# The last down-projection stage of a two-block transformer kernel: dummy matmuls, whole weight buffers, other output queues, f32 sum

## The chip, the cores and the metric

The kernel runs on one core of a Trainium2 chip. A core has TensorE (PE) for matmuls, VectorE (DVE), ScalarE (ACT) and GpSimd (POOL) for element-wise work, SyncE (SP), which here only issues transfers, and 16 DMA engines that move data between HBM and the on-chip memory. The metric is the time of one execution on the device in microseconds. All weights come from HBM once per execution.

## The reference

The program computes two transformer blocks for 256 tokens of width 1024 in float32. Each block has a mixer and a mixture of experts; the change touches the experts of the second block alone. There a router picks for each token one of four groups and in it two of eight experts, each expert is a gated network with a hidden width of 512, and its output is added to the token with a weight:

```python
for e in range(N_EXPERTS_2):                       # 32 experts, hidden width 512
    h = jax.nn.silu(t @ w_gate[e]) * (t @ w_up[e])
    y = y + combine[:, e:e + 1] * (h @ w_down[e]).astype(jnp.float32)
return y.astype(xn.dtype).reshape(B, S, D)         # added to the block's input
```

The weights of the second block's experts are 32 x 3 x 1024 x 512 numbers, 201 MB of the 305 MB that the page counts.

## The kernel before

The experts are taken four at a time, in eight groups (`g` from 0 to 7, function `moe`). Every expert has 32 slots for its tokens, so that the four experts of a group fill the 128 rows of TensorE. A 0/1 matrix S, made from the router's choice, gathers the tokens of a group (L1030); the gate and up products (L1156) work on 32 columns of the array for each expert, with weights that stream in; the hidden values are multiplied on DVE (L1073) and transposed (L1081, ACT copy L1083); the down products (L1089) again take 32 columns for each expert; and `combine` puts the result back to the tokens.

In the second block (`n2` is 4) the down products of a group go in four quarters `q` of 256 output columns. One quarter is one weight buffer of 2 MB, four pieces `c` (128 hidden rows for each of the four experts) of 512 KB; each piece takes four products of 128x32 by 128x256, one for each expert, side by side in the array; the trace shows them as 8 rows in two sets of four, since an f32 product passes twice. The quarter's sum stands in half a PSUM bank (`down_room`). `combine` then splits it into a rounded part `yh` (ACT copy, L1055) and the rest `yl` (DVE subtraction, L1056), and multiplies both by the transposed S for the two halves of the tokens (four matmuls, L1063), which add up over all groups in four PSUM banks (`total_`). Only after the last group (`g == 7`) DVE adds these to X (L1067) and the quarter's 256 columns go out, one DMA for each half of the tokens (L1069): the first three quarters from POOL, the last from ACT.

The weights come through SP's queue in the order in which they are used (`order`, `fetch`, `take`): one DMA of 2 MB for a buffer (L882). The last group's four down quarters come from another array, `w_last_2`, which holds the same numbers with the pieces of a quarter behind each other in a row; each piece is a DMA of its own (L872, 16 in all), so that the products of a piece wait for that piece alone. The DMAs of SP take turns over eight semaphores, so each waits until the one eight before it has landed; a DMA also waits until its buffer is free. PE, ACT, DVE and POOL each work through their instructions in the order of the program; a scheduler fixes that order when the program is built. `held` are the four PSUM banks of the second block for the gate (0), the up (1), the down sums (2) and the small work (3); bank 0 is free once the last gate product has been read.

`keep_warm` (L255) runs matmuls of a matrix of ones whose result nobody reads; before the change it is used in other stages alone.

Of the kernel before, what the change touches and what calls it, by code (L numbers as in the profile page):

```python
# [12 lines left out]
F32 = mybir.dt.float32  # L13
# [3 lines left out]
AF = mybir.ActivationFunctionType  # L17
# [4 lines left out]
P = 128  # L22
# [10 lines left out]
WCOLS = 4096  # L33
# [120 lines left out]
def two_blocks(ctx: ExitStack, tc: tile.TileContext, A: dict, at: dict, out: bass.AP):  # L154
    nc = tc.nc
# [83 lines left out]
    ones_b = const.tile([P, P], BF16, name="ones_b")  # L239
# [59 lines left out]
    def tok(tt):  # L299
        return slice(tt * P, (tt + 1) * P)  # L300
# [217 lines left out]
    w = wload(w_in, 8 * IDX, 8, IDX_W, 2)  # L518
# [24 lines left out]
    for tt in range(NT):  # L543
        ps = bank()
# [34 lines left out]
    ps = bank()  # L579
# [12 lines left out]
    for j in range(4):  # L592
        ps = bank()
        nc.tensor.matmul(ps, con("flip"), relH[j // 2][:, j % 2 * 2:j % 2 * 2 + 2, :].rearrange("p h k -> p (h k)"),
                         start=True, stop=True)
# [30 lines left out]
    ps = bank()  # L626
# [37 lines left out]
    ps = bank()  # L664
# [64 lines left out]
    ps = bank()  # L729
# [3 lines left out]
    for c in range(4):  # L733
# [3 lines left out]
        g = t4([P, 4, T])  # L737
# [63 lines left out]
    def moe(route, gI, br, wgate, wup, wdown, wlast, F, final, total):  # L801
# [63 lines left out]

        pieces = LAST_COLUMNS if n2 == 1 else tuple((r, 1) for r in range(n2))

        def wload_columns(c):
            w, r = stream_tile(), []
            for h, n in pieces:  # L870
                v = w[:, h * 1024:(h + n) * 1024]
                nc.sync.dma_start(v, bass.AP(tensor=wlast.tensor, offset=wlast.offset + c * P * WCOLS + h * 1024,  # L872
                                             ap=[[WCOLS, P], [1, n * 1024]]))
                r.append(v.rearrange("p (e n) -> p e n", e=4))
            return r

        def chunk(what, g, c):
            if what == 2 and g == 7:
                return wload_columns(c)
            src = (wgate, wup, wdown)[what]  # L880
            w = stream_tile()
            nc.sync.dma_start(w, bass.AP(tensor=src.tensor,  # L882
                                         offset=src.offset + (g * src.shape[1] + c) * P * WCOLS,
                                         ap=[[WCOLS, P], [1, WCOLS]]))
            if what == 2 and n2 > 1:
                return [w[:, c_ * 1024:(c_ + 1) * 1024].rearrange("p (e n) -> p e n", e=4) for c_ in range(n2)]
            return w.rearrange("p (e n) -> p e n", e=4)
# [164 lines left out]

        def combine(g, ST, yp, col, n):
            yh, yl = (wtile([P, 512], F32R, tag=tag, bufs=2, level="const")[:, :n] for tag in ("sq", "on"))
            nc.scalar.activation(yh, yp[:, :n], AF.Copy)  # L1055
            nc.vector.tensor_sub(yl, yp[:, :n], yh.bitcast(F32))  # L1056
            for tt in R:
                if final:
                    ps = total_[tt][col // 512][:, col % 512:col % 512 + n]
                else:  # L1060
                    ps = bank()[:, :n]
                for i, y in enumerate((yh, yl)):
                    nc.tensor.matmul(ps, ST[:, tok(tt)], y, start=i == 0 and (not final or (g == 0 and col % 512 == 0)),  # L1063
                                     stop=i == 1, skip_group_check=final)
                xs = X[:, tt, col:col + n]
                if not final or g == 7:
                    nc.vector.tensor_add(xs, xs, ps)  # L1067
                if final and g == 7:
                    (nc.scalar if col >= 768 else nc.gpsimd).dma_start(out[0, tok(tt), col:col + n], xs)  # L1069

        def hidden(gu, sg, sc):
            hid = wtile([P, n2, P], tag="on", bufs=2, level="const")
# [13 lines left out]
        def down(g, hT_, ST):  # L1086
            def step(yp, j, c, w):
                js = slice(32 * j, 32 * j + 32)
                nc.tensor.matmul(yp[js], hT_[:, c, js], w, start=c == 0, stop=c == n2 - 1)  # L1089

            if n2 > 1:
                for q in range(4):
                    w = take(2, g, q)
                    yp = down_room()
                    for c in range(n2):
                        for j in range(4):
                            step(yp[:, :256], j, c, w[c][:, j])
                    combine(g, ST, yp, q * 256, 256)
            elif g < 7:
                yp = [acc() for _ in range(2)]  # L1100
                for c in range(n2):
                    w = take(2, g, c)
                    for hf in range(2):
                        for j in range(4):
                            step(yp[hf], j, c, w[:, j, hf * 512:(hf + 1) * 512])
                for hf in range(2):
                    combine(g, ST, yp[hf], hf * 512, 512)
            else:
                for (h, n), w in zip(pieces, take(2, g, 0)):
                    yp = acc()  # L1110
                    for j in range(4):
                        step(yp[:, :256 * n], j, 0, w[:, j])
                    combine(g, ST, yp, h * 256, 256 * n)
# [220 lines left out]
def prepare(inputs):  # L1334
# [12 lines left out]
    for x in ("", "_2"):  # L1347
        for n in ("w_gate", "w_up", "w_down"):
# [3 lines left out]
            else:  # L1352
                if x:
# [3 lines left out]
    w = a["w_down"][0, 28:].reshape(4, P, D)  # L1357
    arrays["w_last"] = np.concatenate([w[:, :, h * 256:(h + n) * 256].transpose(1, 0, 2).reshape(P, -1)
                                       for h, n in LAST_COLUMNS], 1)[None]
    w = a["w_down_2"][0, 28:].reshape(4, P, 4, 4, 256)  # L1360
    arrays["w_last_2"] = np.ascontiguousarray(w.transpose(3, 1, 2, 0, 4)).reshape(4, P, WCOLS)
    return arrays, at


# [15 lines left out]
```

## Time and profile before

| | us |
|---|---|
| median of 3 runs | 929.75 (928.58 to 931.29) |
| the profiled execution, total | 927.07 |
| its span, first to last instruction | 925.4 |
| mean granted clock of TensorE over the span | 0.92 of 2.4 GHz |
| busy in the span: PE, DVE, ACT, POOL | 760.7, 348.0, 264.7, 172.2 |

The span is what the trace shows; the total of the same execution is 1.67 us longer. A row of the timeline gives start, duration, engine, line, operation, output and inputs, the form, and how many instructions it merges; PE is matmuls, PEld weight loads, an engine's name with q at its end stands for its sequencer, which waits and issues. In brackets is the idle time of the engine before the row and what ended it. The granted clock is a share of 2.4 GHz: 1.00 is 2.4 GHz and 0.50 is 1.2 GHz.

### The profile page before, as it was taken

What the parts mean: (1) busy time and instruction counts of PE and PEld (TensorE: products, weight loads), DVE (VectorE), ACT (ScalarE), POOL (GpSimd) and SP (SyncE); (2) the same over time, 40 slices, a digit from 0 to 9 for tenths busy, and PEclk for the clock granted to TensorE, in tenths of its full rate; (3) what the DMA queues carried; (4) which work ended last, traced back from release to release, by engine and by line L of the source; (5) the groups of instructions that cost most, each with busy time, mean ns of one, the idle gap of its engine ahead of it and who ended that gap; (6) DMA issues with size and microseconds to landing.
All of it is one profiled execution on the core that took longest, in us unless ns stands there. A gap on an engine that the chain in (4) does not pass through costs nothing.

```text
span 925.4 us, 14953 instructions
## 1 busy us (share of the span) xinstructions
PE 760.7 (82%) x6166; PEld 491.3 (53%) x6166; DVE 348.0 (38%) x776; ACT 264.7 (29%) x615; POOL 172.2 (19%) x163
## 2 busy tenths in 40 slices
PE   7989999999998988898999976576486676758666
PEld 6768899986766766786874532132141322313212
DVE  4956465575554558668582110010010101101002
ACT  6446655544211164564651100000000000000000
POOL 3422354575000046522240000000000000000001
PEclk9899999999999998999999997998788968988877
DMA  9561535667599984424669999999999999999996
GB/s 369 228 227 75 200 122 243 252 262 305 216 425 426 419 366 182 188 92 149 259 251 420 428 429 427 425 428 427 426 425 427 427 428 429 428 426 427 426 419 255
DMA packets 26639, 305.04 MB, mean 330 GB/s; under 512 B 2936, under 2 KB 4728, under 8 KB 8512
## 3 DMA queue, kind: packets, MB, share of 16 engines
q1 hardware_dynamic: 25984, 302.93, 79.3%
q8 instruction: 50, 0.82, 0.4%
q0 software_dynamic: 288, 0.79, 0.2%
q10 hardware_dynamic: 288, 0.26, 0.1%
q14 instruction: 29, 0.24, 0.1%
HBM read 302.91 MB, written 1.06 MB: 328 GB/s over the span
## 4 chain that ended last, share of the span: by engine, by line
DMA 44%; PE 17%; DVE 5%; ACT 2%; issue 1%; POOL 1%; DVEq 0%; ACTq 0%; SPq 0%; POOLq 0%
DMA w<-w_up 16%; DMA w<-w_gate 13%; DMA w<-w_down 13%; PE acc L291 6%; DMA w<-w_last 2%; PE ps L1156 2%; PE acc L1156 2%; PE ps L1030 1%; PE ps L1063 1%; PE ps L467 1%; PE acc L1089 1%; POOL wlo L286 1%; PE ps L460 1%; ACT b L446 1%; ACT whi L285 0%
## 5 line engine op out<-in xcount | busy, mean ns | idle before, releaser
L1156 PE MATMUL ps<-w,XT 128*32 128x512 f32 x1024 | 159.3, 748 | 71.9 <-DMA w<-w_up 42.5
L286 POOL TENSOR_TENSOR wlo<-w,whi 128x512 fp32r<-128x512 f32 (+3 forms) x115 | 144.8, 1270 | 190.8 <-ACT whi L285 156.2
L285 ACT ACTIVATE whi<-w 128x512 fp32r<-128x512 f32 (+3 forms) x208 | 120.4, 590 | 91.3 <-PE acc L291 76.9
L1156 PEld LDWEIGHTS ps<-w,XT 128*32 128x32 f32 x1024 | 30.9, 123 | 169.9 <-DMA w<-w_up 68.8
L286 DVE TENSOR_TENSOR wlo<-w,whi 128x512 fp32r<-128x512 f32 (+3 forms) x93 | 71.4, 771 | 54.5 <-ACT whi L285 51.6
L291 PE MATMUL acc<-whi,aT_hi 128*128 128x512 f32 (+3 forms) x240 | 89.2, 377 | 1.0 <-issue 0.7
L291 PE MATMUL acc<-whi,aT_lo 128*128 128x512 f32 (+3 forms) x240 | 87.1, 368 | 0.0
L1089 PE MATMUL ps<-w,pT 128*32 128x256 f32 x1024 | 72.0, 424 | 14.5 <-DMA w<-w_down 11.6
L1069 POOL DMA_DIRECT2D out<-X x6 | 3.4, 577 | 431.4 <-DVE X L1067 431.4
L291 PE MATMUL acc<-wlo,aT_hi 128*128 128x512 f32 (+3 forms) x240 | 70.3, 371 | 5.8 <-DVE wlo L286 3.4
L1083 ACT ACTIVATE pT<-ps 128x128 f32<-128x128 f32 (+1 forms) x16 | 7.0, 437 | 193.3 <-PE ps L1081 193.3
L1030 PE MATMUL ps<-S,X 128*128 128x128 f32 x256 | 39.0, 296 | 23.5 <-DVE XT L1033 12.8
L1030 PEld LDWEIGHTS ps<-S,X 128*128 128x128 f32 x256 | 32.8, 199 | 42.7 <-DVE XT L1033 20.7
L1073 DVE SCALAR_TENSOR_TENSOR on<-ps,sc,sq 128x512 f32<-128x512 f32 x8 | 8.8, 1097 | 123.7 <-PE ps L1156 123.7
L1056 DVE TENSOR_TENSOR on<-ps,sq 128x256 fp32r<-128x256 f32 x32 | 13.6, 425 | 109.3 <-ACT sq L1055 109.3
L1089 PEld LDWEIGHTS ps<-w,pT 128*32 128x32 f32 x1024 | 31.7, 118 | 43.1 <-DMA w<-w_down 14.1
L291 PEld LDWEIGHTS acc<-whi,aT_hi 128*128 128x128 f32 x240 | 46.8, 195 | 11.2 <-issue 3.0
L1033 DVE TENSOR_TENSOR XT<-ps,ck 128x256 f32<-128x256 f32 (+1 forms) x48 | 24.6, 512 | 71.5 <-PE ps L1030 71.4
L291 PEld LDWEIGHTS acc<-wlo,aT_hi 128*128 128x128 f32 x240 | 43.4, 194 | 14.3 <-DVE wlo L286 4.4
L1055 ACT ACTIVATE sq<-ps 128x256 fp32r<-128x256 f32 x32 | 12.3, 384 | 134.6 <-PE ps L1089 134.6
L291 PEld LDWEIGHTS acc<-whi,aT_lo 128*128 128x128 f32 x240 | 46.7, 194 | 6.8 <-issue 0.9
L1045 ACT ACTIVATE ST<-ps 128x256 fp32r<-128x256 f32 x16 | 6.1, 384 | 131.3 <-PE ps L1042 131.3
(288 smaller groups left out, 1190.5 us busy)
## 6 DMA issues: line engine op xcount, KB each, us to landing
w<-w_up SPq DMA_DIRECT2D x40, 2048.0 KB, 39.1
w<-w_gate SPq DMA_DIRECT2D x40, 2048.0 KB, 39.1
w<-w_down SPq DMA_DIRECT2D x35, 2048.0 KB, 39.1
w<-w_in SPq DMA_DIRECT2D x13, 2048.0 KB, 10.3
w<-w_last SPq DMA_DIRECT2D x18, 512.0 KB, 12.8
w<-w_out SPq DMA_DIRECT2D x4, 2048.0 KB, 7.4
w<-w_in SPq DMA_DIRECT2D x2, 1056.0 KB, 19.7
w<-w_in SPq DMA_DIRECT2D x2, 1040.0 KB, 14.6
```

Of the source, the lines that this page charges most:

```text
L285: turn[1] = nc.scalar.activation(r[0], v, AF.Copy)
L286: eng.tensor_sub(r[1], v, r[0].bitcast(F32))
L291: nc.tensor.matmul(out_, a, b, start=start, stop=stop, **kw)
L446: nc.scalar.activation(prob[:, r, s], src, AF.Exp, bias=bias[:, 2 * s + r:2 * s + r + 1], accum_out=sm[:, h:h + 1])
L460: nc.tensor.transpose(ps[:, q * P:(q + 1) * P], prob[:, r, s, tok(kt)], ident)
L467: nc.tensor.matmul(o[:, h * 64:(h + 1) * 64], pT[:, q * P:(q + 1) * P], v[:, kt, h * 64:(h + 1) * 64], start=kt == 0, stop=kt == tt)
L1030: nc.tensor.matmul(ps[:, kk * n:(kk + 1) * n], h[:, tt, kp + kk, :], S[:, tt].rearrange("p e s -> p (e s)"), start=i == 0, stop=i == len(t ...
L1033: nc.vector.tensor_mul(XT[kp * gn // 8][:, k:k + 2, :], ps[:, :2 * n].rearrange("p (k s) -> p k s", k=2), gI[:, kp:kp + 2, None].to_broadc ...
L1055: nc.scalar.activation(yh, yp[:, :n], AF.Copy)
L1056: nc.vector.tensor_sub(yl, yp[:, :n], yh.bitcast(F32))
L1089: nc.tensor.matmul(yp[js], hT_[:, c, js], w, start=c == 0, stop=c == n2 - 1)
L1156: mm = nc.tensor.matmul(gu[i][32 * j:32 * j + 32, :F], XT[k * gn // 8][:, k % (8 // gn), (g % gn) * P + 32 * j:(g % gn) * P + 32 * j + 32] ...
```

## The change

Four things change, all in the last group of the second block's experts.

- The first two down quarters of the last group come as whole buffers of 2 MB from `w_down_2`, like those of the other groups; only the last two come in pieces. The array `w_last_2` now is a copy of those two quarters.
- After each piece's products of the last group, except the last piece of all, PE runs two matmuls of ones (128x512 in bf16) into the free bank `held[0]`: 15 times two. `keep_in_program_order` holds them in their place.
- The output DMAs of the first three quarters are collected and issued by SP, behind the last weight's DMA. Of the last quarter's two, the first stays on ACT and the second goes to POOL.
- The last quarter's sum is not split: ACT copies 128 of its columns and DVE the other 128 in f32, and two f32 matmuls replace the four.

```diff
--- before.py
+++ after.py
@@ -865,17 +865,19 @@
 
         pieces = LAST_COLUMNS if n2 == 1 else tuple((r, 1) for r in range(n2))
 
+        last_load, outs = [None], []
+
         def wload_columns(c):
             w, r = stream_tile(), []
             for h, n in pieces:
                 v = w[:, h * 1024:(h + n) * 1024]
-                nc.sync.dma_start(v, bass.AP(tensor=wlast.tensor, offset=wlast.offset + c * P * WCOLS + h * 1024,
+                last_load[0] = nc.sync.dma_start(v, bass.AP(tensor=wlast.tensor, offset=wlast.offset + (c + wlast.shape[0] - n2) * P * WCOLS + h * 1024,
                                              ap=[[WCOLS, P], [1, n * 1024]]))
                 r.append(v.rearrange("p (e n) -> p e n", e=4))
             return r
 
         def chunk(what, g, c):
-            if what == 2 and g == 7:
+            if what == 2 and g == 7 and c >= n2 - wlast.shape[0]:
                 return wload_columns(c)
             src = (wgate, wup, wdown)[what]
             w = stream_tile()
@@ -1052,21 +1054,36 @@
 
         def combine(g, ST, yp, col, n):
             yh, yl = (wtile([P, 512], F32R, tag=tag, bufs=2, level="const")[:, :n] for tag in ("sq", "on"))
-            nc.scalar.activation(yh, yp[:, :n], AF.Copy)
-            nc.vector.tensor_sub(yl, yp[:, :n], yh.bitcast(F32))
+            plain = final and g == 7 and col == 768
+            if plain:
+                nc.scalar.activation(yh[:, :128].bitcast(F32), yp[:, :128], AF.Copy)
+                nc.vector.tensor_copy(yh[:, 128:].bitcast(F32), yp[:, 128:n])
+            else:
+                nc.scalar.activation(yh, yp[:, :n], AF.Copy)
+                nc.vector.tensor_sub(yl, yp[:, :n], yh.bitcast(F32))
             for tt in R:
                 if final:
                     ps = total_[tt][col // 512][:, col % 512:col % 512 + n]
                 else:
                     ps = bank()[:, :n]
-                for i, y in enumerate((yh, yl)):
+                if plain:
+                    nc.tensor.matmul(ps, ST[:, tok(tt)].bitcast(F32), yh.bitcast(F32), start=False, stop=True,
+                                     skip_group_check=True)
+                for i, y in enumerate(() if plain else (yh, yl)):
                     nc.tensor.matmul(ps, ST[:, tok(tt)], y, start=i == 0 and (not final or (g == 0 and col % 512 == 0)),
                                      stop=i == 1, skip_group_check=final)
                 xs = X[:, tt, col:col + n]
                 if not final or g == 7:
                     nc.vector.tensor_add(xs, xs, ps)
                 if final and g == 7:
-                    (nc.scalar if col >= 768 else nc.gpsimd).dma_start(out[0, tok(tt), col:col + n], xs)
+                    if col < 768:
+                        outs.append((out[0, tok(tt), col:col + n], xs))
+                    else:
+                        (nc.gpsimd if tt else nc.scalar).dma_start(out[0, tok(tt), col:col + n], xs)
+                        if not tt:
+                            with tc.issue_after(last_load[0].ins):
+                                for o, x in outs:
+                                    nc.sync.dma_start(o, x)
 
         def hidden(gu, sg, sc):
             hid = wtile([P, n2, P], tag="on", bufs=2, level="const")
@@ -1095,6 +1112,11 @@
                     for c in range(n2):
                         for j in range(4):
                             step(yp[:, :256], j, c, w[c][:, j])
+                        if g == 7 and q * n2 + c < 4 * n2 - 1:
+                            for _ in range(2):
+                                tc.keep_in_program_order(
+                                    nc.tensor.matmul(held[0], ones_b, ones_b[:, None, :].to_broadcast([P, 4, P]),
+                                                     start=True, stop=True))
                     combine(g, ST, yp, q * 256, 256)
             elif g < 7:
                 yp = [acc() for _ in range(2)]
@@ -1357,8 +1379,7 @@
     w = a["w_down"][0, 28:].reshape(4, P, D)
     arrays["w_last"] = np.concatenate([w[:, :, h * 256:(h + n) * 256].transpose(1, 0, 2).reshape(P, -1)
                                        for h, n in LAST_COLUMNS], 1)[None]
-    w = a["w_down_2"][0, 28:].reshape(4, P, 4, 4, 256)
-    arrays["w_last_2"] = np.ascontiguousarray(w.transpose(3, 1, 2, 0, 4)).reshape(4, P, WCOLS)
+    arrays["w_last_2"] = np.ascontiguousarray(arrays["w_down_2"][7, 2:])
     return arrays, at
 
 
```

TensorE, the last quarter of the last group, before. The names with a number are one buffer each: `w` the weights, `pT` the transposed hidden values, `ps_5628` the down sums, `acc` the sums over the groups, `sq` and `on` the two parts of the split sum.

```order
L1089 MATMUL ps_5628<-w_7629,pT_7528 32x256 x16
L1063 MATMUL acc_5623<-sq_7650,ST_7473 128x256
L1063 MATMUL acc_5625<-sq_7650,ST_7473 128x256
L1063 MATMUL acc_5623<-on_7651,ST_7473 128x256
L1063 MATMUL acc_5625<-on_7651,ST_7473 128x256
L1376 UNCONDITIONAL_BRANCH
```

The same place in the changed kernel, from the third piece of the quarter on; `ps_5626` is the bank `held[0]`.

```order
L1106 MATMUL ps_5628<-w_7641,pT_7528 32x256 x4
L1118 LDWEIGHTS ones_b_82
L1118 MATMUL ps_5626<-ones_b_82 128x512
L1118 LDWEIGHTS ones_b_82
L1118 MATMUL ps_5626<-ones_b_82 128x512
L1106 MATMUL ps_5628<-w_7641,pT_7528 32x256 x4
L1070 MATMUL acc_5623<-sq_7668,ST_7473 128x256
L1070 MATMUL acc_5625<-sq_7668,ST_7473 128x256
L1397 UNCONDITIONAL_BRANCH
```

Between two pieces PE now has two loads of the ones and two matmuls with them; the combine is two matmuls instead of four.

SP's queue from the last up buffer to its end, before:

```order
L882 DMA w_7512<-w_up_2 128x4096
L872 DMA w_7530<-w_last_2 128x1024 x4
L872 DMA w_7563<-w_last_2 128x1024 x4
L872 DMA w_7596<-w_last_2 128x1024 x4
L872 DMA w_7629<-w_last_2 128x1024 x4
L1376 UNCONDITIONAL_BRANCH
```

And in the changed kernel:

```order
L884 DMA w_7512<-w_up_2 128x4096
L884 DMA w_7530<-w_down_2 128x4096
L884 DMA w_7566<-w_down_2 128x4096
L874 DMA w_7602<-w_last_2 128x1024 x4
L874 DMA w_7641<-w_last_2 128x1024 x4
L1086 DMA out<-X_64 128x256 x6
L1397 UNCONDITIONAL_BRANCH
```

Two DMAs of 2 MB stand where eight of 512 KB stood, and six output DMAs follow the last weight. Before these places, the engines' instructions are the same in both kernels but for their line numbers.

## Rows read from the trace of the kernel before

**Rows 1.** The head of the page: span and number of instructions.

```profile
span 925.4 us, 14953 instructions
```

**Rows 2.** The chain of waits from 860 us: start, duration, engine and line.

```profile
896.78 10.61 DMA w<-w_last
...
918.82 1.12 PE ps L1089 x8
...
919.97 0.39 ACT sq L1055
...
920.41 0.86 PE acc L1063 x3
...
921.29 0.42 DVE X L1067
```

**Rows 3.** Stretches: length, busy PE, PEld, DVE, ACT, POOL, clock, DMA share, GB/s.

```profile
860.00:880.00 20.00, 13.09 (x94) 4.47 (x93) 0.61 (x2) 0.52 (x2) 0.00 (x0) 0.83 1.01 427
...
900.00:905.00 5.00, 3.75 (x47) 2.12 (x51) 0.69 (x2) 0.98 (x2) 0.00 (x0) 1.00 1.03 409
...
916.00:918.00 2.00, 2.00 (x20) 0.80 (x24) 0.56 (x2) 0.00 (x0) 1.07 (x2) 0.50 0.40 158
```

**Rows 4.** Timeline of the last group's down stage, from 901 us.

```profile
901.35 1.93 PE L1089 MATMUL ps<-w,pT 128*32 128x256 f32 x32 [0.69 <-ACT pT L1083]
903.41 0.38 ACT L1055 ACTIVATE sq<-ps 128x256 fp32r<-128x256 f32 x1 [2.11 <-PE ps L1089]
...
903.84 0.50 PE L1063 MATMUL acc<-sq,ST 128*128 128x256 f32 x2 [0.56 <-ACT sq L1055]
...
904.74 1.64 PE L1089 MATMUL ps<-w,pT 128*32 128x256 f32 x24
905.47 1.29 POOL L1069 DMA_DIRECT2D out<-X  x2 [422.67 <-DVE X L1067]
...
909.99 0.20 PEld L1089 LDWEIGHTS ps<-w,pT 128*32 128x32 f32 x8 [0.37 <-DMA w<-w_last]
...
911.87 0.20 PEld L1089 LDWEIGHTS ps<-w,pT 128*32 128x32 f32 x8 [1.68 <-DMA w<-w_last]
...
913.14 0.20 PEld L1089 LDWEIGHTS ps<-w,pT 128*32 128x32 f32 x8 [1.08 <-DMA w<-w_last]
...
915.81 0.75 DVE L1067 TENSOR_TENSOR X<-X,acc 128x256 f32<-128x256 f32 x2 [0.67 <-PE acc L1063]
...
916.52 1.07 POOL L1069 DMA_DIRECT2D out<-X  x2 [5.27 <-DVE X L1067]
...
921.29 0.75 DVE L1067 TENSOR_TENSOR X<-X,acc 128x256 f32<-128x256 f32 x2 [0.48 <-PE acc L1063]
921.74 0.86 ACTq L1069 DMA_DIRECT2D out<-X  x2
```

**Rows 5.** DMA issues around 917 and 922.5 us: count, KB each, us to landing.

```profile
out<-X POOLq DMA_DIRECT2D x2, 128.0 KB, 2.6
...
out<-X ACTq DMA_DIRECT2D x2, 128.0 KB, 1.9
```

**Rows 6.** Matmuls of ones before: timeline, and durations (ns min/median/max).

```profile
482.40 3.40 PE L255 MATMUL acc<-ones_b 128*128 128x512 bf16 x15
...
L255 PEld LDWEIGHTS <-ones_b x38: 95/98/291, 227.6 to 486.7; 128*128 128x128 bf16 x38
L255 PE MATMUL acc<-ones_b x38: 376/379/634, 227.8 to 486.9; 128*128 128x512 bf16 x38
```

**Rows 7.** Timeline of PE where 32-column and full-width matmuls alternate.

```profile
843.72 1.06 PE L1156 MATMUL ps<-w,XT 128*32 128x512 f32 x8
844.72 0.66 PE L1081 MATMUL ps<-zk,on 128*128 128x128 f32 x4
845.31 1.06 PE L1156 MATMUL ps<-w,XT 128*32 128x512 f32 x8
```

**Rows 8.** Groups by form over the span: busy us, mean ns, idle before.

```profile
L1083 ACT ACTIVATE pT<-ps 128x128 f32<-128x128 f32 x8 | 2.2, 278 | 29.6 <-PE ps L1081 29.6
```

## The prediction

> **What bounds the kernel now.** I read the chain of waits first. In its last stretch it is DMA almost alone: the weight stream holds it up to 918.82 us, and then come 1.12 us of down products, 0.39 of ACT, 0.86 of combining matmuls and 0.42 of DVE [rows 2]. So the tail counts as weights first, then a serial finish. The span is 925.4 us [rows 1]; the profiled execution took 927.07, 1.67 us more.
>
> The table by stretches says what the engines do in that tail. The granted clock of TensorE is 1.00 (2.4 GHz) at 900 to 905 us and 0.50 (1.2 GHz) at 916 to 918, after weight loads had waited 0.37 to 1.68 us for pieces between 909.99 and 913.14; the DMA engines are full at 900 and only 0.40 busy at 916 to 918 [rows 3, 4]. The timeline gives the steps [rows 4]: a quarter of down products takes 1.93 us at full clock, ACT reads it 0.13 us after its end (901.35 + 1.93 to 903.41) and needs 0.38, the combine starts at 903.84 and the next quarter at 904.74. At half clock the last piece alone takes 1.12 us.
>
> The finish after the last product: the ACT copy, the combine at 920.41, two DVE adds from 921.29 (the second ends at 922.04), two issues on ACT from 921.74, the second starting at about 922.2 and landing 1.9 us later [rows 2, 4, 5]. That is 924.1; the span ends 1.3 us behind it.
>
> **The change, part by part.**
>
> *Two quarters as whole buffers, and the outputs behind the weights.* With 16 KB rows the stream moves 427 GB/s, with the 4 KB rows of the pieces 409 [rows 3]. A quarter is 2.10 MB, 4.92 us against 5.13, so two whole quarters save 0.4 us. The outputs leave POOL's queue, where there are three pairs of one pattern, issued beside the weights [rows 4]. Between 909.99 and 911.87 a piece took 1.88 us, between 911.87 and 913.14 1.27, with 0.5 MB in both [rows 4]; I put the 0.6 down to the first pair. Two pairs can delay weights that still have to land (the third is issued at 916.52), so about 1.2 us goes. The last weight lands at 918.8 - 0.4 - 1.2 = 917.2 (918.8 if I am wrong on the outputs). The six issues that SP takes over stand behind its last weight, so nothing on SP waits for them but the end of the program. The last two depend on the third quarter's adds and would land before 922 us even with a POOL landing (2.6 us), earlier than the last quarter's own outputs. I cost them at nothing.
>
> A whole buffer also has a price: PE can begin a quarter only when all of it has landed. The first lands near 901.7 (the last up buffer had landed by 896.78 [rows 2], plus 4.92), where PE began at 901.35 [rows 4]: 0.35 us. The second is there at 907.0 (its last piece landed two pieces of 1.27 before 909.99 [rows 4], at 907.4, less the 0.4), where PE used to begin it at 904.74 on its first pieces. The early start is lost.
>
> *Dummy matmuls.* After each of the 15 first pieces PE runs two 128x512 bf16 matmuls. Fifteen such matmuls in a row took 3.40 us [rows 6]; less the 0.38 of a single one that is 0.216 each, 0.43 a pair, at full clock. They are in PE's order, so a landed piece waits behind them. A piece's own products are 2 sets of 0.22 (the quarter's 1.93 less a tail of 0.16, over 8 sets), together 0.43. Then there is the change of weights, twice a piece. The row of ones_b has 98 ns for a load [rows 6], and in a place where 32-column products and full-width ones alternate, 843.72 to 845.31 is 1.59 us [rows 7] against 2 sets of 0.43 and four transposes of 0.11, which leaves 0.29 for two changes. So a change costs between 0 (hidden) and 0.15; I take 0.10, the load's own row. One piece is then 0.43 + 0.43 + 0.20 = 1.06 us (bounds 0.86 and 1.15).
>
> The Trainium skill, "TensorE: Matmul & The Clock Gate", Step-by-step, says that PE pulls weight loads ahead of matmuls in flight, so that the next tile's weights load during this one's matmul. By that rule the changes cost nothing and a piece is 0.86. The rows at 843.72 to 845.31 do not agree with it for two shapes that alternate.
>
> A quarter that starts at s has its last products done at s + 3 x 1.06 + 0.60 and lets the next start 0.13 + 0.38 + 0.05 + 0.90 later, at s + 5.24. The dummies behind its fourth piece end at s + 4.24, before the combine could start (s + 4.34), and cost nothing. From 901.7 the first quarter is through at 906.9, so the second starts with its weights at 907.0. The third starts at 912.24 and the fourth at 917.48; by then all weights have landed. The last product ends at 917.48 + 3.18 + 0.60 = 921.26 us, against 918.82 + 1.12 = 919.94 before. PE becomes the bound: +1.3 us.
>
> *The last quarter in f32.* ACT and DVE each copy 128 columns instead of 256 on ACT and a subtraction behind it. ACT's 128x128 row is 278 ns [rows 8]; DVE adds 256 columns in 0.42 [rows 2], and half of them should not take it longer than ACT. I take 0.28 against 0.38, a gain of 0.1 (bounds 0 and 0.15). The subtraction was hidden by the first two combining matmuls, so its removal gives nothing. Two f32 matmuls replace four in f32r. f32 work passes twice, and a pass over 256 columns is the 0.22 of a set, so 4 x 0.22 plus 0.27 of lead and tail is 1.15 us to the last result, where before the second add began 1.22 after the combine's start. Gain 0.07 (bounds -0.2 and +0.2). Together the second add ends at 921.26 + 0.13 + 0.28 + 0.05 + 1.18 + 0.41 = 923.31.
>
> *The last output on POOL.* Before, ACT issued both, and the second landed 2.05 us after the second add. POOL starts its issue later: its pair at 916.52 starts 0.29 after the end of the first add (915.81 + 0.42) [rows 4], and it landed after 2.6 us where ACT's took 1.9 [rows 5]. Part of the 2.6 may be the weights that were still moving, so I take 2.2 between the two rows: 0.29 + 2.2 = 2.5, a loss of 0.45 (bounds 0.1 and 0.85). ACT's own output is earlier and hidden.
>
> The Trainium skill, "DMA: Bandwidth & Descriptors", Latency and other measured facts, gives about 600 ns to the first byte for a queue of ACT or SP and about 1 us for one of POOL. By its 0.4 us the loss would be 0.7 with POOL's later start. The rows, 1.9 and 2.6, point the same way, by more.
>
> **Sum.** Last product +1.3, copy -0.1, combine -0.05, output +0.45, together about +1.7 us: span 927.1, execution 928.8. The median of the runs is 929.75, 2.7 above the profiled execution; I put the +1.7 on it: **931.5 us**.
>
> **Rivals.**
>
> *The weight changes are hidden*, by the skill's rule above. Then a piece is 0.86, the last product ends at 907.0 + 9 x 0.86 + 4.72 = 919.46, 0.5 before now, and the total with -0.15 and +0.45 is -0.2: 929.6 us. For it: in PE's own streams loads do hide. Against it: the 0.29 of rows 7, where shapes alternate as here.
>
> *The clock falls all the same*, the one that ends on the other side. PE still waits for the second quarter until 907.0, and before the change the clock stood at 0.50 at 916 to 918 [rows 3]. If it falls as early as 907, each of about 11 pieces pays double for products and dummies, 0.86 us more, so +9 us: 940. It is over 0.3% slower from 4 such pieces on. Against it: with the dummies PE is near full from 901.7 on, and at 900 to 905, with 3.75 of 5 us busy, it held 1.00.
>
> *PE keeps up with the weights*, so that only the earlier landing counts: last weight 917.2 instead of 918.8, the last piece 0.59 instead of 1.12, -2.1 in all; with -0.15 and +0.45, -1.8: 927.9. It needs the dummies to cost nothing on PE's path, against the 0.43 a pair of rows 6. That the dummies keep the clock and yet bring nothing, since their own time is what the clock gives back, is my forecast itself.
>
> **How the numbers follow.** Forecast 0.68, hidden changes 0.20, falling clock 0.05, PE keeping up 0.07. A difference of 0.3% is 2.8 us, about what a measurement of this kernel can tell from no change. The forecast's own range is from the bounds of the pieces (0.86 to 1.15, -1.8 to +0.8 us) and of the output (-0.35 to +0.4), which seldom meet: 929.6 to 932.7. Medians of three runs of the same kernel wander too (928.58 to 931.29 for the single ones), and the range takes in the two rivals below: 928.6 to 933.4. Slower by over 0.3% (above 932.5) takes the falling clock and the upper end of the forecast, 0.05 + 0.10; faster by over 0.3% (below 927.0) is a part of the last rival and chance, 0.05; the rest, 0.80, is within.
>
> **What would show it.** Right: granted clock 1.00 through 901 to 921; the last weight landing near 917 and no piece of the last quarter waited for; pieces about 1.06 us apart on PE; the second quarter starting at 907; the last product ending near 921.3; the second add about 2.05 us later; the last output landing 2.5 us after that. Wrong: a chain that still ends in the weights' DMA (PE keeps up), pieces at 0.86 (hidden), or a clock of 0.50 in the last quarters.

## The result and the profile after

The changed kernel is slower. In five runs beside five of the kernel before, its median is 936.66 us (932.64 to 940.18) against 930.64. The ratio of the two is 1.0079, with a 95% interval of 1.0051 to 1.0106. On the 929.75 us of before this is +7.3 us (+4.7 to +9.9); the forecast was +1.7 us, and its range ended at 933.4. A later set of ten runs gave 1.0071 (1.0048 to 1.0093). The profiled execution took 932.64 us, the lowest of its five runs, against 927.07 before.

The head of the page and the busy row answer to [rows 1] and to the small table ahead.

```profile
span 930.8 us, 15009 instructions
...
PE 762.6 (82%) x6196; PEld 493.0 (53%) x6196; DVE 346.6 (37%) x776; ACT 264.6 (28%) x615; POOL 170.3 (18%) x158
```

To compare one profile with another, a common zero is needed. Every kernel here has the same instructions up to the products of the last up buffer, but for the matmuls of ones that three of them have in the up stage; and yet these products start between 895.6 and 902.0 us in the fourteen profiles. That spread is none of the change's doing. So I count from that start to the end of the span and call it the tail. In before the start is this row of the timeline:

```profile
896.81 1.92 PE L1156 MATMUL ps<-w,XT 128*32 128x512 f32 x16 [1.29 <-DMA w<-w_up]
```

The tail of before is 925.4 - 896.81 = 28.6 us. After, it is 930.8 - 897.00 = 33.8. Here is the timeline of PE after, from the same row on (start, duration, line, operation, form, count, idle time before and its releaser):

```profile
897.00 3.38 PE L1178 MATMUL ps<-w,XT 128*32 128x512 f32 x16 [1.25 <-DMA w<-w_up]
...
903.01 0.76 PE L1106 MATMUL ps<-w,pT 128*32 128x256 f32 x8 [0.69 <-ACT pT L1100]
903.70 1.03 PE L1118 MATMUL ps<-ones_b 128*128 128x512 bf16 x2
904.66 1.08 PE L1106 MATMUL ps<-w,pT 128*32 128x256 f32 x8
...
907.27 0.60 PE L1118 MATMUL ps<-ones_b 128*128 128x512 bf16 x2
...
909.89 0.64 PE L1106 MATMUL ps<-w,pT 128*32 128x256 f32 x8
...
911.00 0.64 PE L1106 MATMUL ps<-w,pT 128*32 128x256 f32 x8
...
915.25 0.64 PE L1106 MATMUL ps<-w,pT 128*32 128x256 f32 x8
...
920.60 0.64 PE L1106 MATMUL ps<-w,pT 128*32 128x256 f32 x8
...
923.92 0.64 PE L1106 MATMUL ps<-w,pT 128*32 128x256 f32 x8
924.63 0.28 ACT L1059 ACTIVATE sq<-ps 128x128 f32<-128x128 f32 x1 [4.97 <-PE ps L1106]
924.94 0.29 DVE L1060 COPY sq<-ps 128x128 f32<-128x128 f32 x1 [3.59 <-ACT sq L1059]
925.29 1.13 PE L1070 MATMUL acc<-sq,ST 128*128 128x256 f32 x4 [0.72 <-DVE sq L1060]
926.02 0.85 DVE L1077 TENSOR_TENSOR X<-X,acc 128x256 f32<-128x256 f32 x2 [0.79 <-PE acc L1070]
...
927.18 0.74 POOL L1082 DMA_DIRECT2D out<-X  x1 [443.92 <-DVE X L1077]
```

These rows answer to [rows 4]. First look for brackets: behind 903.01 no product of the down stage waits for a transfer. PE is the bound now, as forecast. Then look at the distances. A whole quarter runs from 909.89 to 915.25 and from 915.25 to 920.60, which is 5.36 and 5.35 us. But the first one takes from 903.01 to 909.89, 6.88 us: its first pieces have 1.03 us for two dummies where later ones have 0.60, and 1.08 for products where later ones have 0.64. The stretches say why (columns as in [rows 3]):

```profile
895.00:900.00 5.00, 3.75 (x20) 0.60 (x16) 0.00 (x0) 0.00 (x0) 0.00 (x0) 0.50 1.01 429
900.00:903.00 3.00, 1.04 (x8) 0.42 (x4) 1.09 (x1) 0.60 (x1) 0.00 (x0) 1.00 0.98 415
903.00:905.00 2.00, 1.99 (x14) 0.49 (x18) 0.00 (x0) 0.00 (x0) 0.00 (x0) 0.60 1.00 408
905.00:907.00 2.00, 2.00 (x18) 0.33 (x10) 0.00 (x0) 0.00 (x0) 0.00 (x0) 0.55 0.99 391
907.00:910.00 3.00, 2.97 (x28) 1.08 (x24) 0.54 (x2) 0.39 (x1) 0.00 (x0) 1.00 1.02 406
...
915.00:920.00 5.00, 5.00 (x44) 1.48 (x44) 1.06 (x3) 0.38 (x1) 0.00 (x0) 1.00 0.33 119
```

The granted clock is 0.50 (1.2 GHz) while PE multiplies the last up buffer. It is 1.00 at 900 to 903, where PE is busy for 1.04 of 3 us and otherwise waits for DVE and ACT. It is 0.60 and 0.55 at 903 to 907, in the first pieces, with PE full, and 1.00 from 907 on. The transfers thin out from 915 on. The last weight landed at 916.9 (issued at 906.81, with 10.1 us to landing), and PE finished its last product 7.7 us behind it.

```profile
w<-w_last SPq DMA_DIRECT2D x1, 512.0 KB, 10.1
...
out<-X POOLq DMA_DIRECT2D x1, 128.0 KB, 2.2
```

The second of these rows is the last output (the answer to [rows 5]): issued by POOL at 927.18, landed 2.2 us later.

### The profile page after: what moved, and what is told of

Its sections match the earlier page's. It is cut to its first block, busy times and chain, and to the rows that moved or that the text cites. A ratio compares the mean times of both kernels' runs of the same rounds, so it can differ in the third digit from the quotient of the medians.

```text
span 930.8 us, 15009 instructions
## 1 busy us (share of the span) xinstructions
PE 762.6 (82%) x6196; PEld 493.0 (53%) x6196; DVE 346.6 (37%) x776; ACT 264.6 (28%) x615; POOL 170.3 (18%) x158
## 3 DMA queue, kind: packets, MB, share of 16 engines
HBM read 302.91 MB, written 1.06 MB: 327 GB/s over the span
## 4 chain that ended last, share of the span: by engine, by line
issue 48%; PE 14%; DVE 5%; ACT 2%; POOL 1%; POOLq 0%; ACTq 0%; another core or an unknown queue 0%; DVEq 0%
PE acc L291 6%; PE acc L1178 2%; PE ps L1073 1%; PE ps L467 1%; PE ps L1032 1%; PE acc L1106 1%; POOL wlo L286 1%; PE ps L460 1%; ACT b L446 1%; ACT whi L285 0%; DVE hss L373 0%; PE ps L430 0%; PE ps L389 0%; DVE wlo L286 0%; DVE rs_t L332 0%
## 5 line engine op out<-in xcount | busy, mean ns | idle before, releaser
L1178 PE MATMUL ps<-w,XT 128*32 128x512 f32 x1024 | 154.1, 726 | 74.7 <-DMA w<-w_up 46.9
L1082 POOL DMA_DIRECT2D out<-X x1 | 0.7, 740 | 443.9 <-DVE X L1077 443.9
```

Of the source, the lines that this page charges most:

```text
L1178: mm = nc.tensor.matmul(gu[i][32 * j:32 * j + 32, :F], XT[k * gn // 8][:, k % (8 // gn), (g % gn) * P + 32 * j:(g % gn) * P + 32 * j + 32] ...
```

## The experiments

The theory after the result: the dummies make PE the bound, by their own time and by the first quarter at half clock. The rivals: one of the other three edits costs it, or the delay lies ahead of the down stage. Each part of the change was undone or made alone, then the number of dummies and the clock at the stage's start were changed. All ratios are to the kernel before, run beside it; the tail is that of the one profiled execution.

| kernel | median us | ratio (95%) | tail us |
|---|---|---|---|
| before | 929.76 to 930.64 | 1 | 28.6 |
| the changed kernel | 936.66 | 1.0079 (1.0051 to 1.0106) | 33.8 |
| without dummies | 929.32 | 1.0002 (0.9981 to 1.0024) | 26.8 |
| dummies alone | 935.3 | 1.0073 (1.0047 to 1.0099) | 33.0 |
| whole buffers alone | 929.8 | 0.9995 (0.9974 to 1.0016) | 27.2 |
| output queues alone | 929.02 | 0.9996 (0.9970 to 1.0021) | 27.1 |
| f32 sum alone | 929.55 | 1.0003 (0.9980 to 1.0026) | 27.7 |
| changed, one dummy for two | 932.33 | 1.0029 (1.0010 to 1.0049) | 31.1 |
| before, dummies in the up stage | 929.5 | 0.9987 (0.9969 to 1.0005) | 27.6 |
| changed, dummies in the up stage too | 932.18 | 1.0028 (1.0008 to 1.0048) | 31.3 |
| best, with up dummies | 927.22 | 0.9965 (0.9948 to 0.9983) | 25.9 |
| best, without them | 927.16 | 0.9976 (0.9955 to 0.9998) | 25.9 |
| the changed kernel again | 936.87 | 1.0071 (1.0048 to 1.0093) | 33.7 |
| sum split by rows, no dummies | 929.18 (one run) | - | 26.3 |

**The dummies taken out of the changed kernel, and put alone into the one before.**

```diff
-                        if g == 7 and q * n2 + c < 4 * n2 - 1:
-                            for _ in range(2):
-                                tc.keep_in_program_order(nc.tensor.matmul(held[0], ones_b, ...))
```

> The changed kernel without its 30 dummy matmuls; all else stays. Theory: the dummies, each ahead of landed pieces in PE's order, make PE the bound of the last stage and so let the clock with which PE enters it count in full. Without them a piece is 0.43 us at 2.4 GHz and 0.85 at 1.2 GHz, and PE ends within a microsecond or so of the last weight (916.9 in the changed kernel): 928 to 931 us, 5 to 8 below the changed kernel's 936.7, and a spread over the runs like that of before (about 3 us). Rival one, the whole buffers (PE cannot begin the second quarter before 907): still slower than before, 934 or more. Rival two, the outputs that moved to SP and POOL: still slower, 934 or more.

> The kernel before with the dummy matmuls alone. Theory: PE is the bound, about 1.1 us a piece at 2.4 GHz and twice that at 1.2: 934 to 937 us, most of what the whole change costs, with a wide spread over the runs. Rivals (whole buffers, outputs): within 1 us of before.

Without them the time is that of before, 1.0002; alone they cost 1.0073, nearly the whole. The spreads were not as I expected: the seven runs with the dummies alone lie within 2.8 us, the twelve without them within 6.8. The timeline of PE without dummies:

```profile
904.64 3.43 PE L1106 MATMUL ps<-w,pT 128*32 128x256 f32 x32 [0.69 <-ACT pT L1100]
...
909.50 1.93 PE L1106 MATMUL ps<-w,pT 128*32 128x256 f32 x32
...
917.42 0.64 PE L1106 MATMUL ps<-w,pT 128*32 128x256 f32 x8 [0.20 <-DMA w<-w_last]
918.68 0.64 PE L1106 MATMUL ps<-w,pT 128*32 128x256 f32 x8 [0.62 <-DMA w<-w_last]
```

Its first quarter runs at half clock too (3.43 us against 1.93 for the second), but the last pieces wait for their transfers again, so that the end follows the weights and the slow quarter costs nothing. With the dummies alone, the first products of the four quarters stand at these rows:

```profile
905.33 0.91 PE L1089 MATMUL ps<-w,pT 128*32 128x256 f32 x8 [0.69 <-ACT pT L1083]
...
912.28 0.64 PE L1089 MATMUL ps<-w,pT 128*32 128x256 f32 x8
...
917.63 0.64 PE L1089 MATMUL ps<-w,pT 128*32 128x256 f32 x8
...
922.99 0.64 PE L1089 MATMUL ps<-w,pT 128*32 128x256 f32 x8
```

The first quarter takes 6.95 us, the next two 5.35 and 5.36: the same steps as in the changed kernel, with none of its other edits.

**The three other edits, each alone in the kernel before.**

```diff
...
-            if what == 2 and g == 7:
+            if what == 2 and g == 7 and c >= n2 - wlast.shape[0]:
...
```

> The kernel before with its first two last-group quarters as whole buffers, nothing else. Theory: the weights end 0.4 us earlier, PE begins the second quarter at about 907 instead of 904.7 but has time to catch up: within 1 us of before. Rival (whole buffers are the cause): 933 us or more.

```diff
-                    (nc.scalar if col >= 768 else nc.gpsimd).dma_start(out[0, tok(tt), col:col + n], xs)
+                    if col < 768:
+                        outs.append((out[0, tok(tt), col:col + n], xs))
...
+                        (nc.gpsimd if tt else nc.scalar).dma_start(out[0, tok(tt), col:col + n], xs)
```

> The kernel before with the outputs of the first three quarters on SP behind the last weight and the last output on POOL, nothing else. Theory: the last weight lands about 1.2 us earlier (917.6 instead of 918.8), POOL's last output gives 0.5 back: 929 to 931 us, at most 1 us from before. Rival (the outputs are the cause): 933 us or more.

```diff
+            if plain:
+                nc.scalar.activation(yh[:, :128].bitcast(F32), yp[:, :128], AF.Copy)
+                nc.vector.tensor_copy(yh[:, 128:].bitcast(F32), yp[:, 128:n])
...
```

> The kernel before with the last quarter summed in f32 alone. Theory: the ACT copy shortens by 0.1 us, but DVE's copy waits for ACT's and adds 0.3, and the combine is as long as before: no gain, within 1 us of before. From the last product's end to the second add's end 2.4 us against 2.1 before.

None can be told from before; the medians lie within 0.8 us of each other. The landing of the last weight, counted from the landing of the last up buffer, tells more: 21.6 us with the f32 sum alone, whose stream is that of before (22.0 there), 21.2 with whole buffers, 20.3 with the outputs elsewhere, and 19.9 with both, in one profile each. So whole buffers save about 0.4 us and the outputs about 1.3, the sizes of the forecast. The f32 sum doesn't shorten the finish: from the end of the last product to that of the second add it takes 2.31 us, and 2.14 with the split sum (up-stage dummies alone). DVE's copy starts only when ACT's has ended, as at 924.63 and 924.94 after.

**One dummy for two in the changed kernel.**

```diff
-                            for _ in range(2):
+                            for _ in range(1):
```

> The changed kernel with one dummy matmul after each piece instead of two. Theory: the price is by the dummy on PE's path: a piece is 0.43 + 0.22 + 0.2 to 0.25 for two changes of weights, about 0.88 us instead of 1.11 at 2.4 GHz. From the second quarter on, PE gains 12 x 0.22 = 2.6 us, and some more where the clock is low in the first: 932 to 934.5 us. Rival (the dummies' number does not matter, only that PE switches weights at all): within 1 us of the changed kernel's 936.

```profile
909.87 0.64 PE L1106 MATMUL ps<-w,pT 128*32 128x256 f32 x8
910.44 0.39 PE L1118 MATMUL ps<-ones_b 128*128 128x512 bf16 x1
910.76 0.64 PE L1106 MATMUL ps<-w,pT 128*32 128x256 f32 x8
```

A piece now takes 0.89 us (909.87 to 910.76); with two dummies it was 1.11 (909.89 to 911.00). So a dummy is 0.22, as forecast, and what is left of 0.89 behind one dummy and the products' 0.43 is 0.24: two changes of weights, 0.12 each on average. They don't hide. The ratio falls to 1.0029.

**Dummies in the up stage, in the kernel before and in the changed one.** They keep PE busy where it waits for the last up buffer, and change nothing behind it.

```diff
+                        if final and g == 7 and i == 1:
+                            for _ in range(10 if c < n1 - 1 else 4):
+                                tc.keep_in_program_order(nc.tensor.matmul(held[0], ones_b, ...))
```

> The kernel before with the 34 dummy matmuls in its up stage alone. Theory: its end follows the last weight, so a higher clock at the start of the down stage gives at most 0.5 us at the last piece: within 1 us of before. Rival (the clock at the start bounds the kernel before too): 2 us or more below before.

> The changed kernel with 34 more dummy matmuls in the up stage of the last group (10 behind each of the first three buffers' products, 4 behind the last), where PE waits 2 to 3 us for every buffer. Theory: the changed kernel's slow first quarter (6.9 us where 2.4 GHz gives 5.4, and a start 1.3 us late) and its spread come from a clock of 1.2 GHz as PE enters the down stage. With PE kept busy ahead of it the clock is 1.00 there, the first quarter takes 5.4 us and the median falls by 3 us or more against the changed kernel, to 930 to 933.5. Rival (the clock at the start is no matter, the dummies in the down stage are all): within 1 us of the changed kernel.

In the kernel before they bring nothing that can be told (0.9987, interval to 1.0005). In the changed one they take the ratio from 1.0071 to 1.0028. Its timeline of PE, and a stretch (columns as before):

```profile
897.87 1.92 PE L1178 MATMUL ps<-w,XT 128*32 128x512 f32 x16 [0.61 <-DMA w<-w_up]
...
902.86 0.64 PE L1106 MATMUL ps<-w,pT 128*32 128x256 f32 x8 [1.12 <-DMA w<-w_down]
...
908.28 0.64 PE L1106 MATMUL ps<-w,pT 128*32 128x256 f32 x8
```

```profile
903.00:907.00 4.00, 4.00 (x40) 0.94 (x34) 0.00 (x0) 0.06 (x1) 0.00 (x0) 1.00 0.99 405
```

The clock is 1.00 in the first quarter, which takes 5.42 us (902.86 to 908.28) instead of 6.88, and the last up products take 1.92 instead of 3.38. The first quarter now waits for its whole buffer, landed 902.86 - 897.87 = 5.0 us behind the last up buffer, as forecast (4.92). This is the stage as I had forecast it, and the kernel then costs +2.6 us (+0.7 to +4.5), where I had said +1.7.

**What the other edits are worth without the dummies.** In the changed kernel the down dummies go, the two f32 halves get a buffer and two matmuls each, so that the first half's matmuls don't wait for DVE, and the second last output goes to SP. It was run with the up dummies and without.

```diff
-                nc.vector.tensor_copy(yh[:, 128:].bitcast(F32), yp[:, 128:n])
+                nc.vector.tensor_copy(yl[:, :128].bitcast(F32), yp[:, 128:n])
...
-                        (nc.gpsimd if tt else nc.scalar).dma_start(out[0, tok(tt), col:col + n], xs)
+                        (nc.sync if tt else nc.scalar).dma_start(out[0, tok(tt), col:col + n], xs)
```

> No dummies in the down stage, the 34 in the up stage; whole buffers and outputs behind the weights as in the change; the last quarter's two f32 halves in two buffers (so that DVE need not wait for ACT) and its second output on SP instead of POOL. Theory: PE enters at 2.4 GHz and keeps up with the weights, the end follows the last weight: from the last up buffer's landing to the end about 26.3 us, against 28.6 in the kernel before and 26.8 without any dummies; 926.5 to 929 us, up to 0.4% below before. Rival (low clock does no harm once the dummies are gone from the down stage): the same as the next kernel.

> The kernel just above without the 34 dummies in the up stage. Theory: where the clock is low at the start PE is behind the weights at first and catches up, so it costs at most 1 us against the kernel above: 927 to 930 us. DVE's copy starts together with ACT's instead of 0.3 us after it.

Both beat before by a little, 0.9965 and 0.9976, and can't be told apart: the up dummies aren't needed. They don't keep the clock up for long either. The second quarter with them:

```profile
909.93 3.36 PE L1107 MATMUL ps<-w,pT 128*32 128x256 f32 x32 [1.42 <-DMA w<-w_down]
```

PE had waited 1.42 us for the buffer, and 32 products that take 1.93 us at full clock took 3.36; the end follows the weights, so this costs nothing. The end of the kernel without up dummies:

```profile
917.93 0.64 PE L1107 MATMUL ps<-w,pT 128*32 128x256 f32 x8 [0.62 <-DMA w<-w_last]
918.63 0.28 ACT L1059 ACTIVATE sq<-ps 128x128 f32<-128x128 f32 x1 [4.15 <-PE ps L1107]
918.94 0.29 DVE L1060 COPY on<-ps 128x128 f32<-128x128 f32 x1 [2.77 <-ACT sq L1059]
918.96 0.71 PE L1071 MATMUL acc<-sq,ST 128*128 128x128 f32 x4 [0.40 <-ACT sq L1059]
919.93 0.75 DVE L1078 TENSOR_TENSOR X<-X,acc 128x256 f32<-128x256 f32 x2 [0.70 <-PE acc L1071]
```

The end follows the weights again (0.62 us of waiting for the last piece), and PE starts on ACT's half at 918.96, beside DVE's copy. That copy still begins behind ACT's, although each now writes a buffer of its own; a common start did not come about. From the end of the last product (918.57) to that of the second add (920.68) it is 2.11 us, as with the split sum.

**The last sum split by rows.** What the two copies still have in common is the PSUM bank that they read. Here ACT copies rows 0 to 63 and DVE rows 64 to 127, in one execution of the changed kernel without its down dummies and with the second last output on SP.

```diff
-                nc.scalar.activation(yh[:, :128].bitcast(F32), yp[:, :128], AF.Copy)
-                nc.vector.tensor_copy(yh[:, 128:].bitcast(F32), yp[:, 128:n])
+                nc.scalar.activation(yh[:64].bitcast(F32), yp[:64, :n], AF.Copy)
+                nc.vector.tensor_copy(yh[64:].bitcast(F32), yp[64:, :n])
...
```

> The changed kernel without the down dummies and with the second last output on SP; ACT copies rows 0 to 63 of the last sum (256 columns) and DVE rows 64 to 127, instead of 128 columns each of all rows; the two f32 matmuls as in the changed kernel. A tests where DVE's late start comes from. If it is held because both copies read the same PSUM bank, whatever the rows (theory A): DVE starts within 0.05 us of ACT's end, ACT 0.38 and DVE about 0.4 one behind the other, so that the matmuls start some 0.9 us after the last product's end, 0.2 later than with columns (0.73). If only an overlap in the same rows of a bank counts, as the Trainium skill, PSUM - Partial Sum Buffer, PSUM bank collisions raise a hardware error, has it for parts of 32 rows (theory B): DVE starts within 0.1 us of ACT's start, and the matmuls start 0.5 to 0.6 us after the product's end. The total is no question here: 924 to 932 us by either, one execution.

```profile
906.10 2.87 PE L1106 MATMUL ps<-w,pT 128*32 128x256 f32 x32 [1.13 <-DMA w<-w_down]
...
921.05 0.64 PE L1106 MATMUL ps<-w,pT 128*32 128x256 f32 x8 [0.56 <-DMA w<-w_last]
921.76 0.38 ACT L1059 ACTIVATE sq<-ps 64x256 f32<-64x256 f32 x1 [3.72 <-PE ps L1106]
922.17 0.43 DVE L1060 COPY sq<-ps 64x256 f32<-64x256 f32 x1 [2.44 <-ACT sq L1059]
922.65 1.13 PE L1070 MATMUL acc<-sq,ST 128*128 128x256 f32 x4 [0.96 <-DVE sq L1060]
```

DVE starts at 922.17, 0.03 us behind ACT's end, and the matmuls 0.96 behind the last product: the start that theory A gives. The two copies also write one buffer here, which no run took apart from the bank for rows. (The first row is this kernel's first quarter; more on it below.) The time, 929.18 against 928.84 of before in one execution each, tells nothing.

**The changed kernel once more.**

> The changed kernel once more, for a second profile and more runs. Theory: the spread of its runs has two parts, when the last up buffer lands (897 to 902 us in the profiles of ten kernels that are the same up to there) and the clock in the first quarter. Median 933 to 938 us; from the last up buffer's landing to the end 31.3 (clock 1.00 all through) to 36; pieces at 2.4 GHz 1.10 us again. Rival (the first five runs were an outlier): median within 2 us of before.

```profile
892.05 1.92 PE L1178 MATMUL ps<-w,XT 128*32 128x512 f32 x16 [1.66 <-DMA w<-w_up]
896.95 2.80 PE L1178 MATMUL ps<-w,XT 128*32 128x512 f32 x16 [2.98 <-DMA w<-w_up]
901.84 3.31 PE L1178 MATMUL ps<-w,XT 128*32 128x512 f32 x16 [2.09 <-DMA w<-w_up]
...
907.77 0.83 PE L1106 MATMUL ps<-w,pT 128*32 128x256 f32 x8 [0.69 <-ACT pT L1100]
...
914.67 0.64 PE L1106 MATMUL ps<-w,pT 128*32 128x256 f32 x8
```

The products of the last up buffer start 4.8 us later in this profile than in the first one, and what follows is the same: half clock, a first quarter of 6.90 us, a tail of 33.7. The first two rows are the buffers ahead: 1.92 us for the same 16 matmuls, then 2.80. So the clock moves between its levels inside the up stage. In all, eleven profiles have no up dummies, and in nine of them the last up products take 3.21 to 3.59 us. One of the two with 1.92 is the profile of before from which I predicted; the other is that of the split by rows. For the first quarter before stands alone: in the ten others it was slow, 2.82 to 3.43 us for the 32 products without dummies (2.87 with the split by rows) against 1.93, and 6.2 to 7.0 us from the first quarter's start to the second's with them (4.7 and 5.4 at full clock with one and two).

## Why the prediction was wrong

**The step that failed** is the start of the first quarter and its length: "From 901.7 the first quarter is through at 906.9". Both halves of it take the clock at full level, from the 1.00 at 900 to 905 in before [rows 3]. In the changed kernel the last up products ran at 0.50, so that the first quarter's products waited for what hangs on them (ACT's copy, at 903.01) and not for their buffer; and at 903 to 907 the clock was down again, at 0.60 and 0.55. I can lay out the difference by the steps of the sum, counted from the start of the last up products:

| step | forecast us | after us | more |
|---|---|---|---|
| to the first quarter (901.7 - 896.81; 903.01 - 897.00) | 4.89 | 6.01 | 1.12 |
| first quarter to the second (907.0 - 901.7) | 5.30 | 6.88 | 1.58 |
| the second and the third | 10.48 | 10.71 | 0.23 |
| the last, to its last product (924.56 - 920.60) | 3.78 | 3.96 | 0.18 |
| the finish (927.1 - 921.26; 930.8 - 924.56) | 5.84 | 6.24 | 0.40 |
| sum | 30.3 | 33.8 | 3.5 |

The first two rows hold 2.7 of the 3.5 us. Full clock takes 2.5 of them away: the tail with up dummies is 31.3. The trace of before held a warning: at 860 to 880, in the last down quarter of the group ahead and the gate stage, the mean clock was 0.83 [rows 3]. That quarter and two up buffers just ahead of the last one stand at these rows:

```profile
862.24 3.54 PE L1089 MATMUL ps<-w,pT 128*32 128x256 f32 x32 [1.50 <-DMA w<-w_down]
...
886.98 3.64 PE L1156 MATMUL ps<-w,XT 128*32 128x512 f32 x16 [1.74 <-DMA w<-w_up]
891.87 3.64 PE L1156 MATMUL ps<-w,XT 128*32 128x512 f32 x16 [1.25 <-DMA w<-w_up]
```

The same products take 1.93 and 1.92 us at full clock. So the 1.00 at 900 to 905 was not a property of the stage, as I read it, but one execution's: no other of the eleven profiles without up dummies has it in the first quarter. Before the change the level didn't matter, since the end followed the weights; a stage that PE bounds pays for it.

**The rival of the falling clock** had the right sign and half the mechanism. It put the fall behind 907, where PE was full and the clock stayed at 1.00, and priced 11 pieces; the half clock came ahead of it, and cost about three pieces and the up products. Its 0.05 was argued down from the same single row. Its sum has a slip too: "from 4 such pieces on" leaves out the forecast's own +1.7 us; with it, two such pieces pass 932.5.

**What was right.** PE became the bound, by the dummies alone: 1.0073 with them alone, 1.0002 without. A piece is 1.11 us at full clock, forecast 1.06, bounds 0.86 and 1.15. The changes of weights cost 0.12 each; I had 0.10. By the rule of the Trainium skill, "TensorE: Matmul & The Clock Gate", Step-by-step, that loads are pulled ahead of matmuls in flight where their row groups don't conflict or they go to the background weight buffer, a piece would be an estimated 0.86 with two dummies and 0.65 with one. The traces have 1.11 and 0.89, and the measurement decides: where these two shapes alternate, the changes are not hidden. Whether the page's conditions are met here, no run shows. The last weight landed 2.1 us earlier against the last up buffer than in before's profile and 1.6 earlier than in the two other kernels with its stream that the weights bound (21.5 and 21.6 against 19.9); forecast 1.6. The six outputs on SP cost nothing that can be seen: with them there and POOL's last output, and nothing else changed, the ratio is 0.9996. The last output on POOL landed 2.5 us after the second add (926.87 to 929.4), as forecast.

**Sizes that were off.** The f32 sum was to save 0.15 us and costs 0.17, because DVE's copy runs behind ACT's and not beside it (2.31 against 2.14 us); 0.3 of the 0.4 in the finish is this. (The sum also put in 1.18 us for matmuls that its working has at 1.15; that is no matter here.) DVE is held by a wait: its row names ACT as the releaser, with other columns, with a buffer of its own and with other rows. The Trainium skill, "PSUM — Partial Sum Buffer", PSUM bank collisions raise a hardware error, says that two engines must not touch the same bank in the same 32 rows at one time, reads included, and that a compiler orders them. By it the two copies can't run together, and I hadn't weighed it. The traces agree so far that the program ordered the copies by columns; it did the same for rows (922.17), which the page would let run together. So no run shows what the chip does without that order. The +0.41 in the later quarters is in the main nine pieces of 1.11 for 1.06.

**What stays open.** The table explains the profile's +5.2 us of tail (28.6 to 33.8), of which the forecast had 1.7. The medians differ by 6 to 7. The tail of before's profile is longer than those of the other kernels that the weights bound (26.3 to 27.7, the two best kernels at 25.9 aside): its clock was 1.00 early and 0.50 at the end [rows 3], so that the last piece took 1.12 us [rows 2] where whole buffers alone, at full clock, had 0.64. Most executions of before may end like the others, which would account for the rest; runs without a profile show no tails, so this is argued and not shown. Nor do the runs split the 4 us that the up dummies bring in the changed kernel: its tail fell by 2.4 us, and in the kernel before the same dummies changed the time by -1.2 us, with an interval from -2.9 to +0.5.

## What to carry to other kernels

Dummy matmuls in a stage that transfers pace are free only as long as PE's work, dummies and weight changes included, stays under the pace of the transfers: here three pieces of 1.11 us, the last products and the combine made 5.35 a quarter against 4.9 of transfers, and PE became the bound. Before a stage is made PE-bound, read the clock at its entry in more than one execution, and ask what PE did just ahead of it; a row of 1.00 in a stage that something else bounds says little. Edits of one stage are best tried one by one as well as together: here three of the four together made no difference that can be told (1.0002), and the fourth alone cost 0.7%.

## What the runs showed of the hardware

- A change between products of 32 columns and full-width bf16 matmuls cost PE 0.12 us on average at 2.4 GHz, two changes to a piece (pieces of 1.11 and 0.89 us with two dummies and one, less 0.43 for the products and 0.22 a dummy).
- The clock in the up stage, in which PE waits for every buffer, moved between its levels from one buffer to the next, and not alike in different executions: the last buffer's products took 1.92 us behind a wait of 1.29 in before, and 3.38 behind one of 1.25 after. In the changed kernel it stood at 1.00 at 900 to 903, when PE had little work, and at 0.60 and 0.55 at 903 to 907, when it was full. What sets the moment is open. With dummies in the waits, the last up products (1.92 us) and the first quarter (1.93 us, or 5.42 with down dummies) ran at full clock in all three profiles.
- Two copies out of one half of a PSUM bank, by ACT and DVE, ran one behind the other by 0.03 us, behind a wait that the program has: by columns into one buffer and into two, and by rows. Whether the chip would run them together is not shown.
- The landing of the last up buffer moved between 895.6 and 902.0 us in fourteen executions whose work up to there is the same but for the dummies in three.
